# Row sums on one core: the last store made by two transfers, from two queues

## The chip, the cores and the metric

The kernel runs on one core of one Trainium2 chip. The metric is the device time of one execution in microseconds; a kernel's time is the median over its runs. Beside the runs, one execution was taken by the hardware profiler; its page and its trace are what the tables and the quoted lines below come from. Times in the trace count from the first instruction of the span.

## The reference

```python
def setup_inputs():
    batch, seq, dim = 32, 512, 1024
    return {
        "x": np.random.randn(batch, seq, dim).astype(np.float32),
    }

def reference(x: np.ndarray) -> np.ndarray:
    return np.sum(x, axis=-1).astype(np.float32)
```

The input is 64 MiB of float32, taken as 16,384 rows of 1,024 numbers. The output is one sum for each row, 64 KiB in all.

## The kernel before

The rows are cut into three blocks, of 32, 48 and 48 rows for each of the 128 partitions (`BLOCKS`). Inside a block a partition holds consecutive rows, so a load of 16 rows (a group, `G`) takes one contiguous run of 64 KiB for each partition. There are 8 groups. Three buffers (`xt0` to `xt2`) take the groups in turn; the sums of a block collect in `res0`, `res1` or `res2`, one column for each row.

All loads are issued by SyncE (SP), in the order of the list `loads`, each with a semaphore of its own or of its buffer. The first group comes as one row and then 15 rows. These two loads are taken out of the body of the program and put into its entry block by the code at the end of the file (`EARLY`). Groups 1 to 6 are whole. The last group comes in pieces of 9, 4 and 2 rows (`CUTS`), and its last row in two parts, of 544 and 480 columns (`CUT`), which go to the tile `tail`. From the fourth buffer on, a load waits until VectorE has reduced the group that was in its buffer (line 148).

VectorE reduces most rows (`rows_dve`, one tensor_reduce for several rows) and counts each instruction in the semaphore `vec`. ScalarE takes 7 rows of the last whole group and about half of the rows of the first two pieces and one row of the third (`rows_act`, one activation with an accumulator for each row), counted in `act`. The last row and one row of the third piece are summed by `pairs_dve` on VectorE; the very last instruction of VectorE adds the second part of the last row to the sum of the first (line 129), and writes the last column of `res2`.

The stores are issued by SP as well. Once the third piece has landed and the whole groups are reduced, three early stores go out (line 155): all of `res0`, all of `res1`, and `res2` without its last 16 columns. Then SP waits for the final counts of `vec` and `act` (lines 157 and 158) and issues the last store, the last 16 columns of `res2` (line 159). Its closing is: wait for the three early stores (lines 161 and 162), clear all semaphores but `store` (line 163), wait for `store` and take it back by 16 (line 164). ScalarE has no instruction behind its last row (line 143).

Of the kernel before, what the change touches and what calls it, by code (L numbers as in the profile page):

```python
# [11 lines left out]
G = 16  # L12
BUFS = 3
ACT_ROWS = 7
CUT = 544
CUTS = (0, 9, 13, 15)
EARLY = 2


def row_sums(nc, x: bass.AP, out: bass.AP):  # L20
    P = nc.NUM_PARTITIONS
# [15 lines left out]
    groups, stores = [], []  # L37
# [8 lines left out]
    x_z, res_z, c_z = groups[-1]  # L46
# [3 lines left out]
    pairs = [sbuf(f"pairs{i}", D // 2) for i in range(3)]  # L50

    names = [f"slot{i}" for i in range(BUFS)] + ["first", "piece0", "piece1", "piece2", "tail0"]
    names += ["tail1", "vec", "act", "early0", "early1", "early2", "store"]
    sems = {n: nc.alloc_semaphore(n) for n in names}
    slots = [sems[f"slot{i}"] for i in range(BUFS)]
    vec, act = sems["vec"], sems["act"]
# [3 lines left out]
    count = {"vec": 0, "act": 0}  # L60
# [10 lines left out]
    def rows_act(t, j, n, res, c):  # L71
        for i in range(n):
            v = t[:, (j + i) * D : (j + i + 1) * D]
            nc.scalar.activation(  # L74
                out=v, in_=v, func=COPY, accum_out=res[:, c + i : c + i + 1]
            ).then_inc(act, 1)
            count["act"] += 1
# [15 lines left out]
    for b in range(1, n_groups - 1):  # L93
        x_b, _, c = groups[b]
        loads.append((b, xt[b % BUFS][:, :], x_b[:, c * D : (c + G) * D], slots[b % BUFS]))
        full[b] = (full[b - BUFS] if b >= BUFS else 0) + 16
    for k, (i, j) in enumerate(zip(CUTS, CUTS[1:])):
        src = x_z[:, (c_z + i) * D : (c_z + j) * D]
        loads.append((n_groups - 1, last[:, i * D : j * D], src, sems[f"piece{k}"]))
    for k, (i, j, gap) in enumerate(((0, CUT, 0), (CUT, D, 16))):  # L100
        e = (c_z + G - 1) * D
        src = x_z[:, e + i : e + j]
        loads.append((0, tail[:, i + gap : j + gap], src, sems[f"tail{k}"]))


    freed = {}
    nc.vector.memset(tail[:, CUT + 15 : CUT + 16], 0.0).then_inc(vec, 1)  # L107
    count["vec"] += 1
# [9 lines left out]
    for k in range(2):  # L118
        i, j = CUTS[k], CUTS[k + 1]
        nc.vector.wait_ge(sems[f"piece{k}"], 16)  # L120
# [16 lines left out]
    for k in range(2):  # L137
        i, j = CUTS[k], CUTS[k + 1]
        h = (j - i) // 2
        nc.scalar.wait_ge(sems[f"piece{k}"], 16)  # L140
        rows_act(last, i + h, j - i - h, res_z, c_z + i + h)
    nc.scalar.wait_ge(sems["piece2"], 16)
    rows_act(last, G - 2, 1, res_z, c_z + G - 2)


    for b, dst, src, s in loads:
# [6 lines left out]
    for k, (out_b, res, n) in enumerate(stores):  # L153
        m = n - G if k == len(stores) - 1 else n
        nc.sync.dma_start(out=out_b[:, 0:m], in_=res[:, 0:m]).then_inc(sems[f"early{k}"], 16)
    out_z = stores[-1][0]
    nc.sync.wait_ge(vec, count["vec"])
    nc.sync.wait_ge(act, count["act"])
    nc.sync.dma_start(out=out_z[:, c_z : c_z + G], in_=res_z[:, c_z : c_z + G]).then_inc(sems["store"], 16)

    for k in range(len(stores)):
        nc.sync.wait_ge(sems[f"early{k}"], 16)
    nc.sync.sem_clear(range(numbers[0], sems["store"].num))
    nc.sync.wait_ge(sems["store"], 16).then_inc(sems["store"], -16)


def kernel(tc: tile.TileContext, x: bass.AP, out: bass.AP):
    tc.close()
    tc.compile()  # L169
    nc = tc.nc  # L170
    row_sums(nc, x, out)

    sp = mybir.EngineType.SP
    fn = nc.m.functions[0]
    entry, body = None, None
    for blk in fn.blocks:
        ops = [i for i in blk.instructions if i.engine == sp]
        if entry is None:  # L180
            entry = blk
        elif any(i.opcode == "DMACopy" for i in ops):
            body = blk
            break
    code = list(body.instructions)
    loads = [i for i in code if i.engine == sp and i.opcode == "DMACopy"][:EARLY]
    for load in loads:
        assert not load.sync_info.on_wait
        code.remove(load)
    body.instructions = code  # L190
    code = list(entry.instructions)
    at = next(k for k, i in enumerate(code) if i.engine == sp and i.opcode == "Drain")
    code[at:at] = loads
    entry.instructions = code
# [29 lines left out]
```

## Time and profile before

| | |
|---|---|
| median of 3 runs | 161.14 us (160.81 to 161.16) |
| the profiled execution's own time | 160.73 us |
| its span, first to last instruction | 159.4 us |
| VectorE busy | 121.5 us, 76% of the span |
| ScalarE busy | 17.2 us, 11% of the span |
| read from HBM, written | 67.11 MB, 0.07 MB, 421 GB/s over the span |
| DMA queues in use | one, SP's: 2448 packets |
| the last store, from its issue to its landing | 1.4 us |

The profiled execution's time is 1.33 us more than its span; the span is what the views divide up. Two kinds of instruction need a word. A DMA issue (`SPq ... DMA_DIRECT2D`) is the time in which the sequencer of an engine prepares a transfer; the transfer itself runs afterwards on 16 DMA engines, and "to landing" counts from the beginning of the issue to the last of the 16 semaphore updates. Issues, waits and clears aren't counted as busy time of an engine. In the chain of waits, and in the list of instructions in order of time, the first number is the start, the second the duration, both in us. In the list of waits the numbers are the total, the count and the longest. In the view of one line they are the shortest, median and longest duration in ns.

### The profile page before, as it was taken

To read this page: it belongs to the slowest core of one execution; us is meant where nothing else is said; L and a number is where in the kernel's file an instruction comes from. 1 tells how busy PE (TensorE), PEld (TensorE's weight loads), DVE (VectorE), ACT (ScalarE), POOL (GpSimd) and SP (SyncE) were. 2 spreads that over 40 slices of the span, in tenths; PEclk is the share of its full clock that TensorE was granted. 3 is DMA by queue.
4 is the path that set the end of the run, shared out by engine and by line. 5 is a ranking of instruction groups with operands and counts; after the bars stand their busy time and mean duration, and the time that the engine had idled before them with its cause. 6 is when DMAs were issued, how large, how long until landed. Compare 5 with 4: busy or idle time off the path is not lost.

```text
span 159.4 us, 110 instructions
## 1 busy us (share of the span) xinstructions
DVE 121.5 (76%) x17; ACT 17.2 (11%) x31; POOL 0.2 (0%) x4
## 2 busy tenths in 40 slices
DVE  1100059994799968999499994999949999499685
ACT  3000000000000000000000000000000000494694
POOL 0000000000000000000000000000000000000000
DMA  9988996996997989969969969969979799699994
GB/s 378 493 370 370 493 526 263 526 526 263 526 477 312 526 378 411 526 263 526 526 263 526 526 263 526 526 263 526 460 329 526 312 477 526 296 444 444 387 400 151
DMA packets 2448, 67.18 MB, mean 421 GB/s; under 512 B 784, under 2 KB 912, under 8 KB 1168
## 3 DMA queue, kind: packets, MB, share of 16 engines
q1 hardware_dynamic: 2448, 67.18, 98.2%
HBM read 67.11 MB, written 0.07 MB: 421 GB/s over the span
## 4 chain that ended last, share of the span: by engine, by line
DMA 75%; DVE 22%; SPq 1%; issue 0%
DMA xt<-in_x_dram 50%; DMA tail<-in_x_dram 25%; DVE res L63 22%; SPq L149 1%; DVE pairs L81 0%; DVE res L81 0%
## 5 line engine op out<-in xcount | busy, mean ns | idle before, releaser
L63 DVE TENSOR_REDUCE res<-xt 128x16 f32<-128x16384 f32 (+5 forms) x10 | 119.9, 11994 | 34.1 <-DMA xt<-in_x_dram 34.1
L74 ACT ACTIVATE xt<-xt 128x1024 f32<-128x1024 f32 x15 | 15.6, 1043 | 138.3 <-DMA xt<-in_x_dram 138.3
L74 ACT ACTIVATION_READ_ACCUMULATOR xt<-xt 128x1 f32 x15 | 2.8, 187 | 0.0
L107 DVE MEMSET tail<- 128x1 f32 x1 | 0.1, 59 | 2.0 <-PEq L169 2.0
L74 ACT ACT_TABLE_LOAD x1 | 1.3, 1283 | 1.9 <-PEq L169 1.9
L81 DVE CUSTOM_DVE_ANT_0 pairs<-tail 128x272 f32<-128x272 f32 (+1 forms) x2 | 0.9, 428 | 0.1
L81 DVE CUSTOM_DVE_ANT_0 pairs<-xt 128x512 f32<-128x512 f32 x1 | 0.7, 693 | 0.2 <-DMA xt<-in_x_dram 0.2
L81 DVE DVE_READ_ACCUMULATOR2_ANT res<- 128x1 f32 x2 | 0.2, 82 | 0.0
L208 POOL MEMSET const-bfloat16-1.0<- 128x1 bf16 x1 | 0.1, 102 | 0.0
L208 POOL MEMSET const-uint8-127<- 128x1 uint8 x1 | 0.1, 101 | 0.0
L208 POOL MEMSET const-float32-0.0<- 128x1 f32 x1 | 0.1, 99 | 0.2 <-issue 0.2
L208 POOL MEMSET const-float32-1.0<- 128x1 f32 x1 | 0.1, 98 | 0.0
L81 DVE DVE_READ_ACCUMULATOR2_ANT tail<- 128x1 f32 x1 | 0.1, 82 | 0.0
## 6 DMA issues: line engine op xcount, KB each, us to landing
xt<-in_x_dram SPq DMA_DIRECT2D x1, 7680.0 KB, 21.2
xt<-in_x_dram SPq DMA_DIRECT2D x1, 4608.0 KB, 32.6
xt<-in_x_dram SPq DMA_DIRECT2D x1, 2048.0 KB, 37.0
xt<-in_x_dram SPq DMA_DIRECT2D x1, 1024.0 KB, 39.0
xt<-in_x_dram SPq DMA_DIRECT2D x1, 512.0 KB, 3.5
tail<-in_x_dram SPq DMA_DIRECT2D x1, 272.0 KB, 39.2
tail<-in_x_dram SPq DMA_DIRECT2D x1, 240.0 KB, 39.3
xt<-in_x_dram SPq DMA_DIRECT2D x6, 40.8
```

The lines of the kernel that those rows point to most:

```text
L63: nc.vector.tensor_reduce(out=res[:, c : c + n], in_=t[:, j * D : (j + n) * D].rearrange("p (j d) -> p j d", d=D), axis=X, op=ADD,).then_i ...
L74: nc.scalar.activation(out=v, in_=v, func=COPY, accum_out=res[:, c + i : c + i + 1]).then_inc(act, 1)
L81: nc.vector.tensor_tensor_reduce(out=pairs[:, 0 : h - a], in0=t[:, a:h], in1=t[:, h:b], scale=1.0, scalar=0.0, op0=ADD, op1=ADD, accum_out ...
L107: nc.vector.memset(tail[:, CUT + 15 : CUT + 16], 0.0).then_inc(vec, 1)
L149: nc.sync.dma_start(out=dst, in_=src).then_inc(s, 16)
L208: nc = _bacc.Bacc("TRN2", target_bir_lowering=False, num_devices=1)
```

## The change

The last store is made by two transfers instead of one. SP issues partitions 0 to 95 of the same 16 columns, with the semaphore `store` as before. ScalarE, which has issued nothing until then, waits for its own count and for VectorE's final count behind its last row, and issues partitions 96 to 127, with a new semaphore `late`. SP waits for `late` behind the early stores and before the clear, which now covers `late` too. A helper, `final`, makes both transfers.

```diff
+SPLIT = 96
...
-    names += ["tail1", "vec", "act", "early0", "early1", "early2", "store"]
+    names += ["tail1", "vec", "act", "early0", "early1", "early2", "late", "store"]
...
+    out_z = stores[-1][0]
+
+    def final(queue, p, q, s):
+        dst, src = out_z[p:q, c_z : c_z + G], res_z[p:q, c_z : c_z + G]
+        queue.dma_start(out=dst, in_=src).then_inc(s, 16)
...
     nc.scalar.wait_ge(sems["piece2"], 16)
     rows_act(last, G - 2, 1, res_z, c_z + G - 2)
+    nc.scalar.wait_ge(act, count["act"])
+    nc.scalar.wait_ge(vec, count["vec"])
+    final(nc.scalar, SPLIT, P, sems["late"])
...
-    out_z = stores[-1][0]
     nc.sync.wait_ge(vec, count["vec"])
     nc.sync.wait_ge(act, count["act"])
-    nc.sync.dma_start(out=out_z[:, c_z : c_z + G], in_=res_z[:, c_z : c_z + G]).then_inc(sems["store"], 16)
+    final(nc.sync, 0, SPLIT, sems["store"])
 
     for k in range(len(stores)):
         nc.sync.wait_ge(sems[f"early{k}"], 16)
+    nc.sync.wait_ge(sems["late"], 16)
     nc.sync.sem_clear(range(numbers[0], sems["store"].num))
     nc.sync.wait_ge(sems["store"], 16).then_inc(sems["store"], -16)
```

## The prediction

> **What bounds the kernel now.** I read the page's busy table and queue table first, to see what kind of kernel this is.
>
> ```profile
> span 159.4 us, 110 instructions
> DVE 121.5 (76%) x17; ACT 17.2 (11%) x31; POOL 0.2 (0%) x4
> q1 hardware_dynamic: 2448, 67.18, 98.2%
> ```
>
> One DMA queue, SP's, carries everything, and its packets fill 98.2% of the 16 engines' span: the loads bound the kernel. ScalarE is busy for 11% and issues no transfer. The chain of waits, next, says how it ends.
>
> ```profile
> 118.14 39.32 DMA tail<-in_x_dram
> 157.46 0.05 issue
> 157.51 0.41 DVE pairs L81
> 157.92 0.01 DVE res L81
> ```
>
> The last piece of x lands at 157.46 and VectorE has added it up at 157.92. What comes behind that, 159.4 - 157.92 = 1.48 us, has no name in the chain. It is the last store, and the only stretch that this change touches. The timeline from 156 us on shows who is there:
>
> ```profile
> 156.22 1.30 SPq L155 DMA_DIRECT2D out_dram<-res  x3
> ...
> 157.19 0.19 ACT L74 ACTIVATION_READ_ACCUMULATOR xt<-xt 128x1 f32 x1
> ...
> 157.84 0.08 DVE L81 DVE_READ_ACCUMULATOR2_ANT res<- 128x1 f32 x1
> 157.95 0.33 SPq L159 DMA_DIRECT2D out_dram<-res  x1
> ```
>
> ScalarE is done at 157.19 + 0.19 = 157.38, VectorE at 157.92, and SP begins to issue the store at 157.95. The view of DMA issues has the time to landing, and SP's own waits have what follows:
>
> ```profile
> out_dram<-res SPq DMA_DIRECT2D x2, 16.0 KB, 1.5
> out_dram<-res SPq DMA_DIRECT2D x1, 24.0 KB, 1.6
> out_dram<-res SPq DMA_DIRECT2D x1, 8.0 KB, 1.4
> ```
>
> ```profile
> SPq L164 <- SPq L164: 0.6, 1, 0.6
> SPq L162 <- DMA out_dram<-res: 0.4, 1, 0.4
> ```
>
> The 8 KB store lands 1.4 us after its issue begins, the 24 KB one 1.6: bytes hardly matter, it is a fixed cost. After issuing, SP waits 0.4 us for the early stores (L162), clears the semaphores (L163), and waits 0.6 us more for the last store (L164), so the clear is hidden under the last store's flight. The single records say it to the ns: issue 157.953 to 158.285; first packet 158.779, which is 0.494 after the issue's end; last semaphore packet 158.983; the 16 landings 159.185 to 159.361; the wait 159.378 to 159.395, the end of the span. The packets take 0.20 us of the 1.41.
>
> **The change part by part.** The sum is made against the profiled execution: 160.73 us, a span of 159.40 and 1.33 around it. The median of the runs shown is 161.14 (160.81 to 161.16), 0.41 higher, so I add my difference to the median; 1.33 is kept.
>
> (1) Fewer partitions on SP: 96 rather than 128. The last store has eight 64-byte packets on each of 16 engines, about 7 ns apart in its packet records. Six instead of eight saves 2 x 7 = 0.014 us; ScalarE's 32 partitions, two packets each, save 6 x 7 = 0.042. Whether issue (0.33), the 0.494 to the first packet and the 0.35 or so from semaphore packet to landing depend on partitions isn't shown, since every transfer has 128. From one side nothing; from the other a quarter of 1.41, 0.35 us. I take nothing: bytes per partition go from 64 to 65,536 and a lone issue stays at 327 to 332 ns.
>
> (2) ScalarE's two waits (its own count, VectorE's count). Behind them on ScalarE stands only the new transfer. Its own count is complete at 157.38, 0.54 before VectorE's, so this wait hides under VectorE's last two operations. VectorE's count releases SP and ScalarE together, at about 157.95. Cost nothing; if ScalarE's sums came last, the cover would be gone for SP as well, which waits for both counts already.
>
> (3) ScalarE's issue. No row has a transfer issued by ScalarE. The nearest are SP's: 0.33 alone. But what happens when two are wanted at once? The nearest row is the three early stores, which start at 156.22, 156.61 and 157.09 in the timeline:
>
> ```profile
> L155 SPq DMA_DIRECT2D out_dram<-res x3: 348/432/432, 156.2 to 157.1; - x3
> ```
>
> An issue right behind another costs 0.43 instead of 0.33, and starts come 0.39 and then 0.48 apart. By the packet records the first packet follows each issue's end by 0.49 to 0.50, lone or crowded. So something that the issue uses is still taken when the next begins. If SP and ScalarE share it, the second transfer comes 0.39 to 0.48 behind the first; if not, 0. I take 0.44, the middle of the row, because the crowded issue is the nearest event shown. SP answers a semaphore a little sooner (at 156.2, SP's issue starts 7 ns ahead of ScalarE's activation on the same semaphore), so ScalarE's transfer is the late one. If the hold goes by partitions, it is late by 96/128 of 0.44 = 0.33.
>
> [...]
>
> (4) First use of ScalarE's queue, at the worst place. SP's very first issue took 0.376 against 0.328, and its first packet came 0.63 after the issue's end against 0.49, together 0.19 more, though it reads from HBM where a store reads on chip. From below 0, from above the dearest first use shown on ScalarE, its table load:
>
> ```profile
> 1.91 1.28 ACT L74 ACT_TABLE_LOAD   x1 [1.91 <-PEq L169]
> ```
>
> I take 0 for the sum, 0.19 for the upper end of the forecast, and 1.28 for a rival.
>
> (5) The new wait in SP's closing. It stands before the clear, and so the clear and the wait for the last store are queued behind it. While ScalarE's transfer is the last to land, these run in the open: reaction about 0.016, the wait 0.028, the gap to the next 0.041, the clear 0.051, a gap of about 0.03 and the last wait 0.017, in all 0.18, against 0.034 now from landing to end: 0.15 more. One further wait instruction would make it 0.21. If SP's own transfer lands last by over 0.15, this costs nothing.
>
> (6) 16 more landings. The 16 of the last store come 11.7 ns apart, evenly, as if written one by one. Interleaved on both queues they could end up to 16 x 0.012 = 0.19 later, or nothing where one queue trails; serialized issues keep them apart, so nothing. Loads, VectorE and early stores aren't moved.
>
> Sum for the likeliest case: 0.44 (3) - 0.04 (1) + 0.15 (5) = +0.55. By the profiled execution 160.73 + 0.55 = 161.28; on the median 161.14 + 0.55 = **161.69**. Its own range: SP losing instead, or the hold going by partitions, gives about +0.43; 0.48 + 0.19 + 0.21 - 0.04 gives +0.84: 161.55 to 162.0.
>
> **Rivals.** B, the issues run side by side. For it: two sequencers, and nothing in the trace that says the 0.10 of crowding isn't SP's own. Against: with one queue there is no proof of two. Then ScalarE's transfer lands 0.04 before SP's did, and the clear behind it is uncovered: -0.04 + 0.15 to 0.21 = +0.11 to +0.17, up to +0.36 with (4) or (6) at 0.19: 161.3, not slower as far as can be measured, if these two are nothing.
>
> C, on the other side: the fixed cost isn't fixed but goes by partitions. Place: issue to landing of SP's transfer, 1.41 us. With 96 partitions the issue and the time to the first packet, 0.83 together, shrink by a quarter, 0.21; with the landing 0.35. ScalarE's 32 partitions then land by half a microsecond sooner and hide wait and clear. It decides from the point where issue time falls with partitions and both issues start together. Against: 0.33 at every size; for it: no transfer with fewer than 128 partitions. Time: 161.14 - 0.21 to 0.35 = 160.8 to 160.9.
>
> D, the first use of a second queue is dear, on the chain or around the span: 1.28 in place of 0, or the 1.33 around the span doubled. About 1.28 - 0.04 + 0.15 = +1.4: 162.5. For it, a queue with nothing on it earlier; against, SP's first issue, only 0.05 longer.
>
> That the change doesn't do what it says, for instance that both transfers end on SP's queue, would also cost 0.48 and no more than the forecast; it isn't counted apart.
>
> **How the numbers follow.** Forecast 0.50, B 0.27, C 0.16, D 0.07. A measurement of this kernel tells about 0.2%, 0.32 us, from no change. Faster by more: most of C, 0.11. Within: C's small end 0.05, B without extras 0.18, the forecast's foot 0.05, in all 0.28. Slower: 0.45 of the forecast, 0.09 of B, D: 0.61. The range, 160.9 to 162.1, holds the forecast, B and about half of C, and leaves out D and the other half, some 0.16.
>
> **What would show it.** Step (3): the issue on ScalarE's queue ends 0.3 to 0.5 after SP's, or is longer than 0.33 by that; equal ends at 158.29 mean B. Step (1): SP's issue still 0.33. Step (4): ScalarE's time to landing above 1.4 plus its wait. Step (5): SP's L163 equivalent, the clear, comes after the last landing, not at 158.7; what is left from there to the end is about 0.1 us. Landings of both queues interleaved, later than 159.36, speak for (6). If the span shrinks, C; if the time grows and the span doesn't, the part of D around it. The prediction is wrong if ScalarE's store lands with SP's or before.

## The result, and the profile after

| | before | after |
|---|---|---|
| median of 20 runs each | 160.92 us (160.70 to 161.35) | 161.22 us (160.99 to 161.61) |
| ratio | | 1.0019, 95% interval 1.0012 to 1.0025 |
| profiled execution, its span | 160.73, 159.4 | 161.28, 159.9 |

The change costs 0.30 us, a good half of the forecast's 0.55 and just under the bound of 0.2% that the prediction drew; with 20 runs each it can still be told from none. Of the 0.47 between the forecast's 161.69 and the measured 161.22, 0.22 comes from the starting point (161.14 over three runs, 160.92 over twenty) and 0.25 from the sum. These are the page of the changed kernel and, below it, the end of its instructions in order of time (start, duration):

```profile
span 159.9 us, 113 instructions
...
q1 hardware_dynamic: 2416, 67.17, 97.8%
q10 hardware_dynamic: 48, 0.00, 0.0%
```

```profile
158.04 0.08 DVE L82 DVE_READ_ACCUMULATOR2_ANT res<- 128x1 f32 x1
158.15 0.35 SPq L112 DMA_DIRECT2D out_dram<-res  x1
158.21 0.38 ACTq L112 DMA_DIRECT2D out_dram<-res  x1
```

Queue q10 is ScalarE's; its 48 packets are 32 of data and 16 semaphore updates. The two issues run at the same time: ScalarE's begins at 158.21, while SP's lasts until 158.50. Neither is much longer than the 0.33 of before; the view of the line has them in ns:

```profile
L112 SPq DMA_DIRECT2D out_dram<-res x1: 347/347/347, 158.2 to 158.2; - x1
L112 ACTq DMA_DIRECT2D out_dram<-res x1: 381/381/381, 158.2 to 158.2; - x1
```

What follows them stands in the DMA issues (last column: us from issue to landing) and in SP's own waits:

```profile
out_dram<-res SPq DMA_DIRECT2D x1, 6.0 KB, 1.4
out_dram<-res ACTq DMA_DIRECT2D x1, 2.0 KB, 1.5
```

```profile
SPq L174 <- DMA out_dram<-res: 0.9, 1, 0.9
...
SPq L173 <- DMA out_dram<-res: 0.4, 1, 0.4
```

Before, SP's longest wait in the closing was the last line, L164, with the clear already done. Now it is L174, the wait for `late`, and the clear and the last wait stand behind it. The closing's three instructions, each by its line (shortest, median and longest ns, first and last start):

```profile
L174 SPq EVENT_SEMAPHORE  x1: 27/27/27, 159.8 to 159.8; - x1
```

```profile
L175 SPq EVENT_SEMAPHORE_RANGE_CLEAR  x1: 58/58/58, 159.8 to 159.8; - x1
```

```profile
L176 SPq EVENT_SEMAPHORE  x1: 17/17/17, 159.9 to 159.9; - x1
```

The trace's records of starts, semaphore updates and packets give these to the ns. Below, every time counts from the end of VectorE's last instruction, and the stretch from there to the end of the span is called the tail.

```
                                before    after
SP's issue starts                0.028    0.028
SP's last update lands           1.436    1.410   (issue to landing 1.408, 1.382)
ScalarE's issue starts, ends              0.092, 0.473
ScalarE's last packet                     1.133
ScalarE's last update lands               1.616
end of the span (tail)           1.470    1.816
```

The tail grew by 0.346 us: -0.026 (SP's transfer lands sooner), +0.206 (ScalarE's lands behind it), and 1.816 - 1.616 = 0.200 in place of 0.034 from the last landing to the end, +0.166. The rest of what the two profiled executions differ by isn't the change's: their last loads landed at 157.460 and 157.655. In the profiles of the experiments below, which leave the loads alone, that instant lies anywhere from 157.267 to 157.752, and the tail, not the span, is compared. Around the span nothing grew: 160.73 - 159.395 = 1.335 before, 161.28 - 159.938 = 1.342 after.

So two questions were open: why ScalarE's transfer lands 0.206 behind SP's although its issue ended only 0.098 later, and whether the issues hold each other up at all. The expectations below give the candidates letters: L, all updates go out in one line, 0.012 apart; G, the two issues share the something that an issue uses in the prediction's step (3), so that the 0.049 by which ScalarE's issue is longer than SP's of before (0.381, 0.332) is a wait for SP's; Q, ScalarE's queue is slow by itself; and P, from the run with four partitions on, two updates on the same DMA engine keep a distance.

### The profile page after: what moved, and what is told of

Read it like the earlier page. It is cut to its first block, busy times and chain, and to the rows that moved or that the text cites. A ratio compares the mean times of both kernels' runs of the same rounds, so it can differ in the third digit from the quotient of the medians.

```text
span 159.9 us, 113 instructions
## 1 busy us (share of the span) xinstructions
DVE 121.5 (76%) x17; ACT 17.2 (11%) x31; POOL 0.2 (0%) x4
## 4 chain that ended last, share of the span: by engine, by line
DMA 75%; DVE 22%; SPq 1%; issue 0%
DMA xt<-in_x_dram 50%; DMA tail<-in_x_dram 25%; DVE res L64 22%; SPq L161 1%; DVE pairs L82 0%; DVE res L82 0%
```

## Experiments

All diffs are against the changed kernel unless said otherwise. The two runs with four partitions and the one with the on-chip copy leave part of the output out and ran once each, for their traces. Ratios are to the kernel before, with their 95% intervals.

**Both transfers on SP's queue.**

```diff
-    nc.scalar.wait_ge(act, count["act"])
-    nc.scalar.wait_ge(vec, count["vec"])
-    final(nc.scalar, SPLIT, P, sems["late"])
...
     final(nc.sync, 0, SPLIT, sems["store"])
+    final(nc.sync, SPLIT, P, sems["late"])
```

> Both transfers on SP's queue, 96 partitions and then 32. The tail, from the end of VectorE's last instruction to the end of the span, is 1.47 us before and 1.82 with the change. All theories: the second issue starts 0.39 after the first and takes 0.43, so the late transfer lands about 1.84 after the first issue's start, and the closing (0.17 from landing to end in place of 0.03) lies in the open: tail 2.05 to 2.10, time about 0.6 us (0.37%) over before. This is the price of serialized issues; with the change at 0.35 in its profile, a tail here no longer than 1.85 would mean that ScalarE's queue saved nothing.

```profile
158.09 0.82 SPq L112 DMA_DIRECT2D out_dram<-res  x2
```

Ratio 1.0040 (1.0028 to 1.0053), tail 2.056. The second issue started 0.390 after the first and took 0.426; its transfer landed 0.436 behind the first. This is what serialized issues cost: 2.056 - 1.470 = 0.586, nearly the forecast's 0.55. The changed kernel doesn't pay it, since its tail is 0.24 shorter. The first issue, with nothing beside it, took 0.347 here too, so the 0.015 above the 0.332 of before aren't owed to ScalarE's company. What they are owed to isn't shown; the first early store of before, alone as well, took 0.348.

**ScalarE issues the whole store.**

```diff
-    nc.scalar.wait_ge(act, count["act"])
     nc.scalar.wait_ge(vec, count["vec"])
-    final(nc.scalar, SPLIT, P, sems["late"])
+    nc.scalar.wait_ge(act, count["act"])
+    final(nc.scalar, 0, P, sems["late"])
...
-    final(nc.sync, 0, SPLIT, sems["store"])
...
-    nc.sync.wait_ge(sems["store"], 16).then_inc(sems["store"], -16)
```

> ScalarE issues the whole last store, 128 partitions; SP issues none, and nothing else is in flight beside it. ScalarE's issue took 0.381 us in the change, from packet to landing 0.48, against 0.332 and 0.35 to 0.38 on SP before. Theory L (landings of two transfers go out one behind the other, and ScalarE's sequencer is a little slower by itself): issue 0.36 to 0.39, last semaphore packet to last landing 0.35 to 0.39. [...] Rival Q (ScalarE's queue is slow by itself, at its first use): issue 0.38, packet to landing 0.48 even alone. Tail by L and G 1.55 to 1.65 (closing in the open, no last wait behind it), by Q 1.70 to 1.75.

```profile
158.06 0.37 ACTq L112 DMA_DIRECT2D out_dram<-res  x1
```

Issue 0.370, last packet to last landing 1.105 to 1.486 = 0.381, tail 1.624, ratio 1.0007 (0.9998 to 1.0016). With nobody to wait for, ScalarE's issue is some 0.04 longer than SP's 0.332 of before, and its updates, alone too, land as fast as SP's did (1.058 to 1.436 = 0.378). The issue is 0.011 shorter than in the change. (The tail holds 0.138 of closing, since here too the clear stands behind the landing.) That takes away both G (0.011 at most) and a second queue that is slow by itself as causes of the 0.206.

**The wait for ScalarE's transfer behind the clear.**

```diff
-    names += ["tail1", "vec", "act", "early0", "early1", "early2", "late", "store"]
+    names += ["tail1", "vec", "act", "early0", "early1", "early2", "gone", "late", "store"]
...
-    nc.scalar.wait_ge(vec, count["vec"])
+    nc.scalar.wait_ge(vec, count["vec"]).then_inc(sems["gone"], 1)
...
-    nc.sync.wait_ge(sems["late"], 16)
-    nc.sync.sem_clear(range(numbers[0], sems["store"].num))
+    nc.sync.wait_ge(sems["gone"], 1)
+    nc.sync.sem_clear(range(numbers[0], sems["late"].num))
     nc.sync.wait_ge(sems["store"], 16).then_inc(sems["store"], -16)
+    nc.sync.wait_ge(sems["late"], 16).then_inc(sems["late"], -16)
```

> The wait for ScalarE's transfer stands behind the clear, beside the wait for SP's own transfer; for that ScalarE tells SP by a semaphore of its own when it has passed its waits, and SP waits for this before the clear. If the closing in the open costs what it seems to (0.20 from last landing to end against 0.034): tail 1.82 - 0.14 = 1.68, time 0.16 us above before (ratio 1.0010). If issue and landing cost it all, tail 1.82 and ratio 1.0019.

SP's waits now end with two in a row, both behind the clear:

```profile
SPq L176 <- SPq L176: 0.5, 1, 0.5
...
SPq L177 <- SPq L177: 0.2, 1, 0.2
```

Tail 1.629, ratio 1.0013 (1.0004 to 1.0022). From the last landing (1.595) to the end it is 0.034 again, so this mend takes back the whole 0.166 of the closing. L177 shows what is left: 0.2 us in which SP waits for ScalarE's transfer alone.

**ScalarE's waits in the other order.**

```diff
-    nc.scalar.wait_ge(act, count["act"])
     nc.scalar.wait_ge(vec, count["vec"])
+    nc.scalar.wait_ge(act, count["act"])
```

> ScalarE's two waits are in the other order, so that its own count, complete early, is the separate wait, and the transfer itself waits for VectorE, as on SP. Its issue should start within 0.02 us of SP's rather than 0.064 behind. Theory L (landings in one line, 32 at 0.0117 us behind the first): ScalarE's packets come 0.06 earlier, but its last landing is bound by the line, about 0.36 to 0.37 after SP's first; tail 1.79 to 1.82. Rival G: the issue gets longer by the 0.05 to 0.06 that it starts earlier (0.43), tail 1.82. Rival Q (fixed 0.48 from packet to landing): tail 1.75 to 1.76.

```profile
158.21 0.35 SPq L112 DMA_DIRECT2D out_dram<-res  x1
158.22 0.39 ACTq L112 DMA_DIRECT2D out_dram<-res  x1
```

The issues start 0.004 apart and still take 0.347 and 0.391. ScalarE's is 0.021 over what it took alone, so one issue doesn't queue behind the other. ScalarE's last packet is sent at 1.084 instead of 1.133, and yet its last update lands at 1.623 instead of 1.616. Tail 1.823, ratio 1.0024 (1.0012 to 1.0037). So within these 0.05 us ScalarE's landing isn't set by when ScalarE issues. Whether it is set by SP's transfer, the next runs ask.

**Four partitions for ScalarE.**

```diff
-    final(nc.scalar, SPLIT, P, sems["late"])
+    final(nc.scalar, SPLIT, SPLIT + 4, sems["late"])
```

> ScalarE's transfer takes partitions 96 to 99 alone, so it ends in 4 semaphore updates rather than 16; partitions 100 to 127 of the last 16 columns are left out. Nothing else differs from the change. In the change ScalarE's 16 updates landed 1.434 to 1.616 us after VectorE's end, from right behind SP's 16 (1.252 to 1.410). Theory L (updates go out in one line): 4 updates, last at 1.42 to 1.48, tail 1.62 to 1.68. Rival P (on each DMA engine the second queue's update comes 0.18 after the first queue's): engines 0 to 3, 1.43 to 1.48, tail the same. Rival Q (fixed 0.48 from packet to landing on the second queue): 1.48 to 1.55. If the number of updates doesn't matter: 1.616, tail 1.82.

Tail 1.586, and the updates came in an order that nothing above foresaw:

```
ScalarE's 4:              1.271  1.283  1.315  1.366
SP's last 4 of 16:        1.455  1.465  1.493  1.552
difference                0.184  0.182  0.178  0.186
```

SP's other 12 updates landed from 1.261 to 1.418, as in the change. ScalarE's four landed first, in SP's midst, and four of SP's came later, each 0.18 behind one of ScalarE's. A line 0.012 apart doesn't do that; P's 0.18 fits, if either queue can be first. The records name no DMA engine: the pairs are made by the order of landing and by the count, four of SP's sixteen behind ScalarE's four, and that both of a pair are on one engine, as P has it, isn't shown. The expectation had P's distance right and its order wrong.

**ScalarE's queue used early.**

```diff
+    nc.scalar.wait_ge(vec, freed[1])
+    out_b, res, n = stores[0]
+    nc.scalar.dma_start(out=out_b[:, 0:n], in_=res[:, 0:n]).then_inc(sems["early0"], 16)
...
-    for k, (out_b, res, n) in enumerate(stores):
+    for k, (out_b, res, n) in list(enumerate(stores))[1:]:
```

> The store of the first block is moved from SP's queue to ScalarE's, where it is issued when the block is reduced, near 58 us; the last store is split as in the change, so ScalarE's part of it is no longer the first use of that queue. ScalarE's last issue took 0.381 in the change, 0.370 alone, against 0.332 to 0.347 on SP. If first use costs the difference, it falls to 0.33 to 0.35 and the first issue near 58 us shows 0.37 or more; if ScalarE's sequencer is slower by itself, it stays at 0.37 to 0.39. In both, landings and closing are the change's: tail 1.78 to 1.82, time 0.2 to 0.35 us above before, and nothing around the span grows (1.33 to 1.35).

At 58 us SP issues a load and ScalarE the moved store, at the same moment; at the end both issue their parts of the last store:

```profile
58.21 0.33 SPq L164 DMA_DIRECT2D xt<-in_x_dram  x1
58.22 0.39 ACTq L143 DMA_DIRECT2D out_dram<-res  x1
```

```profile
157.96 0.35 SPq L112 DMA_DIRECT2D out_dram<-res  x1
158.03 0.35 ACTq L112 DMA_DIRECT2D out_dram<-res  x1
```

First use 0.39, second use 0.353, where the change's first use with the same 32 partitions took 0.381: here the first use cost ScalarE's queue some 0.03 us, and what is left above SP's issues (0.332 to 0.347) is 0.02 or less. It doesn't matter for the end: packets are out at 1.109 rather than 1.133, the last update lands at 1.614. Tail 1.813, ratio 1.0025 (1.0007 to 1.0042).

**Sizes swapped.**

```diff
-SPLIT = 96
+SPLIT = 32
```

> SP stores partitions 0 to 31 and ScalarE 32 to 127. If issue or flight went by partitions, SP's issue would fall from 0.347 to about 0.25 and its transfer would land 0.3 to 0.9 us sooner. If they are fixed: SP's issue 0.33 to 0.35, its last landing 1.37 to 1.41 after the issue's start, ScalarE's behind it; tail 1.80 to 1.86, time 0.25 to 0.4 us above before.

```profile
out_dram<-res SPq DMA_DIRECT2D x1, 2.0 KB, 1.3
out_dram<-res ACTq DMA_DIRECT2D x1, 6.0 KB, 1.5
```

SP's issue of 32 partitions took 0.340 and its last update landed 1.357 - 0.028 = 1.329 after the issue's start, against 1.382 for 96 and 1.408 for 128. The fixed cost was fixed but for 0.08 us between 128 and 32 partitions, and rival C falls. ScalarE's updates landed 0.18 to 0.21 behind SP's again, paired by their order, although it carried three times the bytes. Tail 1.752, ratio 1.0013 (1.0002 to 1.0023).

**Four partitions each.** Against the run with the waits swapped:

```diff
-    final(nc.scalar, SPLIT, P, sems["late"])
+    final(nc.scalar, SPLIT, SPLIT + 4, sems["late"])
...
-    final(nc.sync, 0, SPLIT, sems["store"])
+    final(nc.sync, 0, 4, sems["store"])
```

> SP stores partitions 0 to 3 and ScalarE 96 to 99, each with 4 semaphore updates, and ScalarE's waits are swapped so that both issues start together; the last 16 columns of the other partitions are left out. Theory L (one line of updates, 0.012 apart): both land within a few updates, ScalarE's last 1.30 to 1.37 us after VectorE's end (SP's last at 1.28 to 1.30). Rival P (the second queue's update 0.18 after the first's on the same DMA engine, however few there are): ScalarE's last at 1.43 to 1.48.

```
SP's 4:                   1.095  1.117  1.131  1.173
ScalarE's 4:              1.277  1.293  1.309  1.357
difference                0.182  0.176  0.178  0.184
```

The bounds were set on the idea that SP's updates would land as late as in the change, at 1.28 to 1.30. They landed at 1.173, so the absolute 1.357, inside L's bounds, says nothing; the difference decides. SP's updates took 1.173 - 0.844 = 0.329 from last packet to last landing. At that pace ScalarE's last packet, at 0.891, would have landed at 1.22, and four updates in a line behind SP's would end by then too. They came 0.18 behind SP's with only eight updates in all. Theory L falls and P's distance stands, by the difference and not by the bounds that were written down.

**The closing alone.** Against the kernel before:

```diff
-    nc.sync.sem_clear(range(numbers[0], sems["store"].num))
-    nc.sync.wait_ge(sems["store"], 16).then_inc(sems["store"], -16)
+    nc.sync.wait_ge(sems["store"], 16)
+    nc.sync.sem_clear(range(numbers[0], numbers[0] + len(numbers)))
```

> The kernel before, with one store on SP's queue, but the wait for it stands ahead of the clear, so that the clear runs behind the last landing. If the closing in the open is worth what the change's trace says: tail 1.47 + 0.10 to 0.15 = 1.57 to 1.62 (wait, gap, clear, and no wait after it, as in the run with ScalarE alone, where landing to end was 0.138), time 0.10 to 0.15 us over before. If something else hides it: tail 1.47, ratio 1.000.

Tail 1.579, which is 0.109 more, as expected from the trace; ratio 1.0005 (0.9996 to 1.0014), too small for the runs' times alone to tell from none.

**ScalarE's transfer stays on chip.** Against the run with the waits swapped:

```diff
+    copy = sbuf("copy", G)
...
-    final(nc.scalar, SPLIT, P, sems["late"])
+    nc.scalar.dma_start(out=copy[SPLIT:P, :], in_=res_z[SPLIT:P, c_z : c_z + G]).then_inc(sems["late"], 16)
```

> ScalarE's transfer copies partitions 96 to 127 into another tile on chip instead of writing them out; those partitions' last 16 columns are left out of the output. Waits swapped, both issues start together; SP's transfer is the change's. In the runs so far the second update on a DMA engine landed 0.18 to 0.2 after the first, and with two writes to HBM in flight. If the two updates on one engine are kept apart whatever the data go to: one set of 16 still lands 0.18 after the other, later set's last at 1.55 to 1.65. If it is the second write to HBM that has to be acknowledged: ScalarE's updates land early, before 1.2, and SP's last at 1.41 as in the change.

Inconclusive. The issue took 0.537 and the first packet came only at 1.229, 0.31 later than with the store. ScalarE's updates landed from 1.530 to 1.729, 0.28 to 0.33 behind SP's. Its first packet was sent 0.17 after SP's last (1.229, 1.059), and its last update landed 0.343 after the packet of that update, no later than the 0.381 of ScalarE alone. The two sets were sent too far apart to answer the question, so what makes up the 0.18 remains open; the expectation's "on a DMA engine" is again the author's reading of the order, for the records name none.

## Why the prediction came out as it did

**Bound and place: right.** VectorE's end, the tail behind it and nothing else is where the change acts; loads and the 1.33 around the span stayed.

**Step (3), the failed one.** "I take 0.44, the middle of the row, because the crowded issue is the nearest event shown." The row was of one sequencer issuing twice, and it was read as a property of something that two sequencers would share. In these runs two sequencers hardly held each other up: 0.33 and 0.39 at 58 us started 0.004 apart, 0.347 and 0.391 at the end started 0.004 apart, against 0.370 for ScalarE alone. The crowding came with SP's own issues alone, 0.426 for the second in the run on one queue, and there it is charged: the second transfer landed 0.436 late. Here ScalarE's issue ended 0.098 behind SP's, of which 0.064 is the separate wait for VectorE's count. That wait was put at nothing in step (2), and even so neither it nor the issue's length reached the end: the runs that took them away ended no sooner (1.823, 1.813 against 1.816). The prediction's sign for this step, an end 0.3 to 0.5 after SP's, came out at 0.098 and so spoke for B. Its last sign, a store that lands with SP's or before, stayed silent, because ScalarE's store lands late for another reason.

With both issuing at once, ScalarE's issue shows at most 0.02 of waiting, 0.391 against 0.370 alone: if SP and ScalarE share something, an issue holds it for far less than its own length. ScalarE's issue ended 0.371 sooner than SP's second one in the run on one queue (0.473, 0.844), and 0.24 of that reached the end (1.816, 2.056).

**Step (6), the term missed.** Put at nothing because serialized issues would keep the updates apart, and bounded by 0.19 on the idea of a line of updates. What was measured is 0.206 between the two last landings, close to that bound by luck: it isn't from a line, and the landings weren't interleaved either, which was the prediction's sign for this step. Paired by their order, the updates of one queue landed 0.18 to 0.21 behind those of the other, and still 0.18 when there were only four. By these runs it is this, and not the issue, that sets ScalarE's landing; what makes the distance, no run shows. An estimate of what it alone costs: at the 0.381 from last packet to landing of ScalarE alone, the transfer would have landed at 1.133 + 0.381 = 1.514 instead of 1.616, so 0.10 of the 0.206 is owed to it. The other 0.10 would be left without it, 0.075 of it packets sent later than SP's (1.133, 1.058); while the order holds, sending them sooner gains nothing, as the run with the waits swapped shows.

**Step (5), right.** 0.15 predicted, up to 0.21; 0.166 measured, and given back whole when the clear went first.

**Steps (1) and (4), right in size.** Fewer partitions saved 0.026 on SP's transfer, against a bound of 0.35. (The lone issue wasn't quite as steady as written there: the first early store took 348 ns, outside 327 to 332.) First use cost about 0.03 (0.381 against 0.353), against bounds of 0 and 0.19; rival D doesn't occur, inside or around the span.

**The sum.** In place of 0.44 - 0.04 + 0.15 = 0.55 it is 0.206 - 0.026 + 0.166 = 0.346 in the profiles and 0.30 in the medians. What came true is rival B with its extra (6), written as "+0.11 to +0.17, up to +0.36": B had a chance of 0.27, 0.09 of it with extras. The direction held, and the range 160.9 to 162.1 has the measured 161.22 in it, but not for the forecast's reason: the largest term read one engine's crowding as shared and wasn't paid, and a term put at nothing made good nearly half of it.

No version here beats the kernel before. With the clear first, the split still ends 0.16 later in its tail: one transfer has one set of 16 updates, and the last update of the second set came 0.19 to 0.21 behind that of the first in every version split 96 to 32 or 32 to 96 over both queues, both writing to HBM.

## What to carry to other kernels

A row in which one engine's issues crowd each other says nothing of two engines' issues: here SP's second issue took 0.426 behind its first, and ScalarE's beside SP's 0.391, against 0.370 alone. For that, find two engines that issue at once, or price both cases alike. Splitting this small last store over two queues took only 0.026 us off SP's flight, since issue to landing hardly depended on its size (1.33 us for 32 partitions, 1.41 for 128), and it added a second completion, 0.206 later, and a second wait, with 0.166 of closing behind it. Put whatever the closing must do before the wait for the transfer that lands last: here that alone was worth 0.17 us.

## What the runs showed of the hardware that was not expected

The semaphore updates of two small stores of different queues, paired by their order, landed 0.18 to 0.21 us apart, ScalarE's first in the run with four partitions for it and SP's first in the others; the records name no DMA engine. A transfer of four partitions took ScalarE 0.55 us to issue, and SP 0.33, in the same run. An on-chip copy of 32 partitions took ScalarE 0.537 to issue and 0.66 more to its first packet, against 0.391 and 0.50 for the store of the same partitions. And the store that ScalarE issued at 58 us, 16 KB in the midst of the loads, landed only after 24 us:

```profile
out_dram<-res ACTq DMA_DIRECT2D x1, 16.0 KB, 24.0
```

The packet records show how it went out. Until 78 us the store's 128-byte packets went out in rounds of 16, 2.42 us apart, and one load packet of 65,536 bytes took 2.418. So a round took as long as one such load packet; what orders the packets of the two queues, the records don't show.
